# Other durations in the model by which a hybrid decoder layer's instructions are put in order

## The chip, the core and the metric

The kernel runs on one core of one Trainium2 chip. Its time is device microseconds (us) of that core, from the first instruction to the last, for one launch that computes the whole step. A core has the engines PE (TensorE, matmuls and transposes; its weight loads are listed apart as PEld), DVE (VectorE), ACT (ScalarE), POOL (GpSimd) and SP (SyncE, which here issues nearly all DMA transfers). Each engine works through its own list of instructions strictly in the order in which the program holds them, and waits at an instruction until the semaphores it names have been raised by the others.

## What is computed

One layer of a hybrid decoder, for a prompt of 512 tokens with 16 learned meta tokens ahead of it, and for 8 sequences that decode one token each (536 tokens in all, width 1024):

```
h  = RMSNorm(x)
x += W_o( sig(gate_a) * W_a(GatedDeltaNet(h)) + sig(gate_b) * W_b(GLA(h)) )
x += W_down( gelu(causal_dwconv3(RMSNorm(x) W_up)) * (RMSNorm(x) W_gate) )
y  = RMSNorm(x)
```

`h @ w_in` is a product with 7192 output columns that gives queries, keys, values and gates of both mixers. The delta mixer (4 heads of 128) works in chunks:

```
M = where(strict, (k*beta) k^T * decay, 0);  T = inverse(I + M)       # triangular solve
u = T (v*beta);  w = T (k*beta*exp(G));  v_new = u - w S
o = (q*exp(G)) S + (q k^T * decay) v_new;  S = S*exp(gl) + (k*exp(gl-G))^T v_new
```

The GLA mixer (4 heads, 128x256 state) does the same without the inverse but with a decay per key column. The ConvFFN has 2816 hidden columns. The decode samples take one recurrent step on the states given. Everything is float32; new states and convolution rows are returned too.

## The kernel before

**Big products.** Each is cut into jobs of 128 output columns. A job loads its weights by DMA into a tile `wr` (128x8x128, three buffers), splits each half of it into a rounded part `wh` (cast, ACT) and the rest `wl` (subtraction, DVE; four buffers each), and adds up `hTh*wh + hTl*wh + hTh*wl` in a PSUM tile `g`. These are matmuls of 128x128 weights on 260 to 268 columns; a job with 1024 rows of weights is 48 of them. When it is complete, its result is evacuated, for the columns of `w_in` by ACT or DVE into `zt` and from there to DRAM (`z_d`). The jobs' `g` tiles share few buffers, so a later job can begin only when an earlier one's tile has been evacuated. The second half of the program is the ConvFFN, which is hardly anything but such jobs.

**Small work.** The mixers' chunk work is cut into many small matmuls (16, 32, 64 or 128 rows or columns) into PSUM tiles `s`, with transposes (`tr`, by a matmul with the identity). They are threaded into the stream of the jobs. The inverse is done in two stages. For all 16 diagonal blocks of 32x32 at once DVE solves row by row: 31 pairs of `tensor_tensor`, a product `tmpb<-Ab,Xb` and a sum `Xb<-Xb,tmpb`, each on the result of the one before. The blocks come to it by DMA through DRAM (`nb_d`, `Ab`), and its results go back by DMA through DRAM: four `xb_d<-Xb` and then four `NT<-xb_d`. From there PE combines blocks of 32 to 64 (`s<-NT 32x32`, `s<-Uu,Pm`) and of 64 to 128 (`s<-NT 64x64`, `s<-Uu,Pg`), with copies by ACT (`Pm`, `Pg`, `Uu`) and transposes by DVE (`Uu<-NT`) between the steps; then the chunks follow one after another.

**What sets the order.** Nothing is issued while the body runs. Each operation is recorded by `Plan.add` with its engine, a modelled cost, a latency `lat` (0.17 unless given) and a priority (a due time by a simple clock of `Driver`). `Plan.emit`, called twice (once for the mixers, once for the FFN), then plays the whole program through in time: it takes the engine that is free first, and among its operations whose inputs are there (`need`) the one of the highest priority; it models the SP queue, the ACT tables, PE's two clocks, the rotation of buffers, and a charge where PE goes from full-size to small operations (0.09) or back (0.3). The order of start times found is the order in which each engine's instructions stand in the program. So a modelled duration changes nothing that is computed; it can only move an instruction ahead of or behind others. `need` is set in two places, at L183 (inputs that an earlier `emit` already placed) and at L265 (all others): the time at which the input's operation is modelled to be finished, `lat` included, and without `lat` if both are on PE.

**Where the modelled costs are.** `mm` (L414) and `tr` (L425) give PE's. All operations of the other engines get theirs in `Engine` (L360).

Of the kernel before, what the change touches and what calls it, by code (L numbers as in the profile page):

```python
# [16 lines left out]
P = 128  # L17
# [58 lines left out]

class Op:
    __slots__ = ("eng", "cost", "lat", "fn", "pri", "func", "need", "deps", "users", "tiles", "finish", "left", "duty", "small", "lock", "hold")


def boxes(ap):
# [36 lines left out]
class Plan:  # L118
# [50 lines left out]
    def emit(self):  # L169
# [4 lines left out]
        for op in ops:  # L174
            op.left = 0
            if op.eng in ("sync", "gpsimd"):
                op.need = op.pri[0] - 100.0
            for d in op.deps:
                if d.finish is None:
                    op.left += 1  # L180
                    d.users.append(op)
                else:
                    op.need = max(op.need, d.finish - (d.lat if d.eng == op.eng == "PE" else 0.0))  # L183

        def offer(op):
            for n in op.tiles:
                if n not in alloc:
                    waiting[self.tag[n]].setdefault(n, []).append(op)
                    return
                op.need = max(op.need, alloc[n])  # L190
            cand.setdefault(op.eng, []).append(op)

        def grant(tag):
            while self.next[tag] < len(self.order[tag]) and self.slots[tag]:
                n = self.order[tag][self.next[tag]]
                self.slots[tag].sort()
                alloc[n] = self.slots[tag].pop(0)
                self.next[tag] += 1
                for op in waiting[tag].pop(n, []):
                    offer(op)  # L200
# [7 lines left out]
        while len(done) < len(ops):  # L208
            best = None
            for e, l in cand.items():  # L210
                if l:
                    t = max(self.free.get(e, 0.0), min(o.need for o in l))
                    if best is None or t < best[0]:
                        best = (t, e)
            if best is None:
                raise RuntimeError("no instruction can go on")
            t, e = best
            able = [o for o in cand[e] if o.need <= t + 0.01]
            if e == "PE" and self.idle > 0.3:
                able = [o for o in able if o.duty > 0.9 * o.cost] or able  # L220
            op = min(able, key=lambda o: o.pri)
            if e == "PE" and op.small != self.small:

                same = [o for o in able if o.small == self.small and (self.small or t < op.need + op.hold)]
                op = min(same, key=lambda o: o.pri) if same else op
            if e in WAITERS:
                soon = [o for o in cand[e] if o.pri[0] < op.pri[0] - 2.0 and o.need < t + WF * op.cost]
                if soon:
                    op = min(soon, key=lambda o: o.need)
                    t = max(t, op.need)  # L230
            cand[e].remove(op)
            cost = op.cost
            if e == "sync":
                t = max([t, self.hw] + self.queue[-8:-7])
                self.hw = t + 0.475
                self.bw = max(self.hw + 0.65, self.bw) + cost
                op.finish = self.bw + 0.9
                self.queue.append(op.finish)
                self.free[e] = max(t + 0.06, self.hw - 0.3)
            else:  # L240
                if op.func and not (self.set and op.func in self.set):
                    s = [x for x in ACT_SETS if op.func in x]
                    if s:
                        cost += 1.28
                        self.set = s[0]
                if e == "PE":
                    while t >= self.tick + 3.413:
                        self.warm, self.cols, self.tick = self.cols >= 1.275, 0.0, self.tick + 3.413
                    self.cols += op.duty
                    self.idle = max(self.idle + 0.5 * (t + cost - self.free.get(e, 0.0)) - op.duty, -0.3)  # L250
                    if self.small != op.small:
                        cost += TO_PARTS if op.small else TO_WHOLE
                    self.small = op.small
                    if not self.warm:
                        cost += op.duty
                if op.lock:

                    t = max(t, self.port[e == "vector"])
                    self.port[e != "vector"] = t + cost
                self.free[e] = t + cost  # L260
                op.finish = t + cost + op.lat
            done.append((t, len(done), op))
            for u in op.users:
                u.left -= 1
                u.need = max(u.need, op.finish - (op.lat if op.eng == u.eng == "PE" else 0.0))  # L265
                if u.left == 0:
                    offer(u)
            for n in op.tiles:
                live[n] -= 1
                if live[n] == 0:  # L270
                    tag = self.tag[n]
                    if n not in self.held:
                        self.slots[tag].append(op.finish)
                        grant(tag)
# [119 lines left out]
def body(ctx, tc, I, O):  # L394
    nc = tc.nc
    drv = Driver()
# [17 lines left out]
    def mm(out, lhsT, rhs, start=True, stop=True):  # L414
        n, m = rhs.shape[-1], lhsT.shape[-1]
        k = lhsT.shape[0]
        small = rhs.dtype != F32R and (m <= 64 or k <= 64)
        if rhs.dtype == F32R:
            cost = max(n / 2400 + .0117, .112 * m / P, .025)
        else:  # L420
            cost = n / 2400 + .005 if m <= 32 or k <= 32 else .058 if m <= 64 and n <= 64 else max(n / 600 + .005, .222 * m / P)
        duty = (n / 2400 if rhs.dtype == F32R else n / 2400 + .007 if m <= 32 else n / 600) * k / P
        drv.matmul(cost, out, [lhsT, rhs], lambda: nc.tensor.matmul(out=out, lhsT=lhsT, rhs=rhs, start=start, stop=stop), duty, small)  # L423

    def tr(out, in_):  # L425
        k = in_.shape[0]
        drv.matmul(max(.03, .110 * k / P), out, [in_], lambda: nc.tensor.transpose(out, in_, ident[:k, :k]), 2 * k / 2400 * k / P, k <= 64)  # L427

    def S_(name="s"):
        p, n = ps_pool[-1]  # L430
# [116 lines left out]
    def run(jobs, W):  # L547
        while jobs:
# [11 lines left out]
            for bs in ((0,), (1,)) if len(group) > 1 else (range(group[0].nb),):  # L560
                for j, ps in zip(group, acc):
                    n, K = 0, sum(k for _, k in j.srcs)
                    cols = halves(j.c0, j.n) if j.halves else spans(j.c0, j.n) if j.nb > 1 else [(0, j.n)]

                    pv = ps.rearrange("p a b -> p (a b)")[:, 512 - cols[0][1]:][:, :j.n] if j.nb > 1 else ps[:, 0, :j.n]
                    for i, (s, kk) in enumerate(j.srcs):
                        if (j, i) not in ws:
                            ws[j, i] = W.next()
                        for k in range(kk):
                            hi, lo = ws[j, i][k // 4]  # L570
                            ah, al = j.acts(n + k)
                            drv.poll(drv.earliest(hi, lo, ah, al, *([ps] if n + k == 0 else [])))
                            for p, (w, a) in enumerate(((hi, ah), (hi, al), (lo, ah))):
                                for b in bs:
                                    mm(pv[:j.M, cols[b][0]:cols[b][1]], w[:, k % 4, :j.M], a[:, j.c0 + cols[b][0]:j.c0 + cols[b][1]],
                                       start=n + k == 0 and p == 0, stop=n + k == K - 1 and p == 2)
                        n += kk
                    if bs[-1] == j.nb - 1:
                        with ahead(EV):
                            j.evac(pv[:j.M])  # L580
                        drv.poll()
# [4 lines left out]
    ident = cst[:, C_ID:C_ID + P]  # L586
# [76 lines left out]
    def warm_up():  # L663

        ps = S_("warm")
        for _ in range(28):
            mm(ps[:, :P], scm[:, :P], scm[:, :P])

    def turn_weights():
        ps = S_()  # L670
        tr(ps[:, :8], nmr)
        dve.tensor_copy(nrm_mix, ps[:, :8])
# [55 lines left out]
    def small_operands():  # L728
# [21 lines left out]
        for m in range(12):  # L750
            tr(ps[:, m * 28:(m + 1) * 28], csr[:28, m * P:(m + 1) * P])
# [1074 lines left out]
```

## Time and profile before

| | |
|---|---|
| time, median of 3 runs | 986.65 us (986.44 to 990.56) |
| the profiled execution | 986.13 us, its span 984.4 us |
| granted TensorE clock, mean over the span | 0.995 of full speed |
| PE busy | 968.4 us |
| DVE / ACT / POOL busy | 606.6 / 463.3 / 185.3 us |
| DMA | 135.48 MB, 138 GB/s over the span |

Matmuls are pipelined, so a row of the timeline shows a start and the time until the end of the last of its matmuls, which reaches past the start of the next row. What a matmul takes of PE's time is the distance from start to start. In brackets stands the time in which the engine did nothing ahead of the instruction, and what ended it. Of float32 matmuls with small tiles the trace holds two records for one instruction.

### The profile page before, as it was taken

What the parts mean: (1) busy time and instruction counts of PE and PEld (TensorE: products, weight loads), DVE (VectorE), ACT (ScalarE), POOL (GpSimd) and SP (SyncE); (2) the same over time, 40 slices, a digit from 0 to 9 for tenths busy, and PEclk for the clock granted to TensorE, in tenths of its full rate; (3) what the DMA queues carried; (4) which work ended last, traced back from release to release, by engine and by line L of the source; (5) the groups of instructions that cost most, each with busy time, mean ns of one, the idle gap of its engine ahead of it and who ended that gap; (6) DMA issues with size and microseconds to landing.
All of it is one profiled execution on the core that took longest, in us unless ns stands there. A gap on an engine that the chain in (4) does not pass through costs nothing.

```text
span 984.4 us, 21968 instructions
## 1 busy us (share of the span) xinstructions
PE 968.4 (98%) x9022; PEld 950.4 (97%) x9022; DVE 606.6 (62%) x1197; ACT 463.3 (47%) x905; POOL 185.3 (19%) x278
## 2 busy tenths in 40 slices
PE   9999999999999999999999999999999999999996
PEld 8999999998999999999999999999999999999996
DVE  4879867883457867324754447777776766433254
ACT  6566654745446455244643337344443433232343
POOL 4100116101222244012211122111122111000000
PEclk9999999999999999999999999999999999999998
DMA  7643322445123232656655536477655554433354
GB/s 235 184 116 88 87 66 65 133 130 142 34 77 87 79 90 83 188 161 204 204 174 150 162 110 182 139 237 213 199 157 156 166 152 126 126 118 93 111 143 140
DMA packets 208681, 135.48 MB, mean 138 GB/s; under 512 B 14353, under 2 KB 196392, under 8 KB 208308
## 3 DMA queue, kind: packets, MB, share of 16 engines
q1 hardware_dynamic: 208580, 134.07, 46.9%
q8 instruction: 71, 1.16, 0.5%
q14 instruction: 30, 0.25, 0.1%
HBM read 112.26 MB, written 21.98 MB: 136 GB/s over the span
## 4 chain that ended last, share of the span: by engine, by line
PE 81%; DMA 1%; issue 0%; DVE 0%; ACT 0%; SPq 0%; POOLq 0%; POOL 0%; ACTq 0%
PE g L423 71%; PE s L423 8%; PE s L427 1%; DMA xb_d<-Xb 0%; DMA NT<-xb_d 0%; PE on L423 0%; ACT zt L389 0%; PE pk L423 0%; SPq L389 0%; PE pq L423 0%; POOLq L1822 0%; ACT gat L389 0%; DVE wy L389 0%; DVE ga L389 0%; POOL rfb L389 0%
## 5 line engine op out<-in xcount | busy, mean ns | idle before, releaser
L389 ACT CAST wh<-wr 128x512 fp32r<-128x512 f32 (+1 forms) x300 | 183.1, 612 | 312.3 <-PE g L423 297.4
L389 DVE TENSOR_TENSOR wl<-wr,wh 128x512 fp32r<-128x512 f32 (+1 forms) x296 | 203.6, 698 | 177.1 <-ACT wh L389 175.4
L423 PE MATMUL g<-hTh,wh 128*128 128x268 f32 (+3 forms) x768 | 160.8, 288 | 1.0 <-ACT zt L389 1.0
L423 PE MATMUL g<-hTl,wh 128*128 128x268 f32 (+3 forms) x768 | 161.7, 288 | 0.0
L423 PE MATMUL g<-hTh,wl 128*128 128x268 f32 (+3 forms) x768 | 160.9, 288 | 0.0
L423 PE MATMUL g<-h2l,wh 128*128 128x260 f32 x704 | 142.8, 284 | 0.0
L423 PE MATMUL g<-h2h,wh 128*128 128x260 f32 x704 | 142.0, 282 | 0.0
L423 PE MATMUL g<-h2h,wl 128*128 128x260 f32 x704 | 142.0, 283 | 0.0
L423 PEld LDWEIGHTS g<-hTh,wh 128*128 128x128 f32 x768 | 120.0, 189 | 3.6 <-issue 1.9
L423 PEld LDWEIGHTS g<-hTl,wh 128*128 128x128 f32 x768 | 120.9, 189 | 1.7 <-issue 1.2
L423 PEld LDWEIGHTS g<-hTh,wl 128*128 128x128 f32 x768 | 119.8, 189 | 1.5 <-issue 1.2
L423 PEld LDWEIGHTS g<-h2h,wl 128*128 128x128 f32 x704 | 109.3, 189 | 0.1
L423 PEld LDWEIGHTS g<-h2h,wh 128*128 128x128 f32 x704 | 108.6, 189 | 0.1
L423 PEld LDWEIGHTS g<-h2l,wh 128*128 128x128 f32 x704 | 108.6, 189 | 0.0
L423 PE MATMUL g<-actl,wh 128*128 128x260 f32 (+2 forms) x352 | 79.3, 284 | 0.0
L423 PE MATMUL g<-acth,wh 128*128 128x260 f32 (+2 forms) x352 | 78.2, 283 | 0.0
L423 PE MATMUL g<-acth,wl 128*128 128x260 f32 (+2 forms) x352 | 77.9, 282 | 0.0
L423 PEld LDWEIGHTS g<-actl,wh 128*128 128x128 f32 x352 | 57.7, 188 | 0.1
L423 PEld LDWEIGHTS g<-acth,wl 128*128 128x128 f32 x352 | 57.3, 188 | 0.0
L423 PEld LDWEIGHTS g<-acth,wh 128*128 128x128 f32 x352 | 57.2, 188 | 0.0
L389 ACT ACT_TABLE_LOAD x34 | 43.6, 1283 | 7.4 <-DVE na L389 3.4
L389 POOL TENSOR_TENSOR E<-kb,E 128x256 f32<-128x256 f32 (+1 forms) x32 | 25.5, 807 | 56.5 <-DVE E L389 31.9
(362 smaller groups left out, 1675.5 us busy)
## 6 DMA issues: line engine op xcount, KB each, us to landing
wr<-in_w_in SPq DMA_DIRECT2D x56, 512.0 KB
wr<-in_w_ffn_in SPq DMA_DIRECT2D x44, 512.0 KB
wr<-in_w_ffn_out SPq DMA_DIRECT2D x20, 512.0 KB
z_d<-zt SPq DMA_DIRECT2D x28, 261.0 KB
Sg<-in_state_gla SPq DMA_DIRECT2D x8, 512.0 KB
wr<-in_w_b_out SPq DMA_DIRECT2D x8, 512.0 KB
wr<-in_w_o SPq DMA_DIRECT2D x8, 512.0 KB
So<-in_state_gla SPq DMA_DIRECT2D x8, 512.0 KB
```

Source lines behind the costliest of these rows:

```text
L389: self.drv.issue(self.key, cost, out, ins, 2.2 if self.key == "sync" else 0.17, lambda: f(*args, **kw), func, lock)
L423: drv.matmul(cost, out, [lhsT, rhs], lambda: nc.tensor.matmul(out=out, lhsT=lhsT, rhs=rhs, start=start, stop=stop), duty, small)
L427: drv.matmul(max(.03, .110 * k / P), out, [in_], lambda: nc.tensor.transpose(out, in_, ident[:k, :k]), 2 * k / 2400 * k / P, k <= 64)
```

## The change

A function `Op.saved` says by how much earlier than others a user on the same engine sees a result. On PE this is `lat`, as before. On DVE, ACT and POOL it is `lat` less 0.03, where nothing was taken off before; for users on another engine, and for SP, nothing, as before. It stands in both places at which `need` is set. The cost of float32 matmuls on PE is changed for operands of 64 or fewer rows or columns: with 32 or fewer contraction rows (`k`) and more than 32 output rows (`m`) the cheap formula no longer holds, and a 64x64 product is set to 0.12 instead of 0.058. A transpose costs at least 0.05 instead of 0.03.

```diff
+    def saved(self, user):
+
+        return 0.0 if user.eng != self.eng or self.eng == "sync" else self.lat - (0.0 if self.eng == "PE" else 0.03)
...
-                    op.need = max(op.need, d.finish - (d.lat if d.eng == op.eng == "PE" else 0.0))
+                    op.need = max(op.need, d.finish - d.saved(op))
...
-                u.need = max(u.need, op.finish - (op.lat if op.eng == u.eng == "PE" else 0.0))
+                u.need = max(u.need, op.finish - op.saved(u))
...
-            cost = n / 2400 + .005 if m <= 32 or k <= 32 else .058 if m <= 64 and n <= 64 else max(n / 600 + .005, .222 * m / P)
+            cost = n / 2400 + .005 if m <= 32 else .12 if m <= 64 and n <= 64 else max(n / 600 + .005, .222 * m / P if k > 32 else 0.0)
...
-        drv.matmul(max(.03, .110 * k / P), out, [in_], lambda: nc.tensor.transpose(out, in_, ident[:k, :k]), 2 * k / 2400 * k / P, k <= 64)
+        drv.matmul(max(.05, .110 * k / P), out, [in_], lambda: nc.tensor.transpose(out, in_, ident[:k, :k]), 2 * k / 2400 * k / P, k <= 64)
```

The instructions themselves stay the same, but for two more loads of an ACT table (36 instead of 34). Their order changes on every engine. On PE it changes in the mixers' part; from the last jobs of that part on, which is from about 487 us of the span before, the order on PE is the same row for row. Lines below L80 stand 4 further down in the changed kernel (L389, L423, L427 become L393, L427, L431).

SP, at the end of the diagonal blocks' solve. `xb0` to `xb3` carry the solve's results to DRAM, `NT` brings them back, `z7` and `z8` are the results of the jobs with tiles `g_547` and `g_554`, `wr` the weights of later jobs, `er_d` a row of the decode samples. Before:

```order
L389 DMA z7_d_78<-zt_553 128x522
L389 DMA wr_555<-in_w_in 128x8x128
L389 DMA z8_d_79<-zt_562 128x522
L389 DMA xb0_d_125<-Xb_410 16x1024
L389 DMA xb1_d_126<-Xb_410 16x1024
L389 DMA xb2_d_127<-Xb_410 16x1024
L389 DMA xb3_d_128<-Xb_410 16x1024
L389 DMA wr_564<-in_w_in 128x8x128
L389 DMA NT_405<-xb0_d_125 32x16x32
```

And now:

```order
L393 DMA wr_555<-in_w_in 128x8x128
L393 DMA xb0_d_125<-Xb_410 16x1024
L393 DMA xb1_d_126<-Xb_410 16x1024
L393 DMA xb2_d_127<-Xb_410 16x1024
L393 DMA z7_d_78<-zt_553 128x522
L393 DMA xb3_d_128<-Xb_410 16x1024
L393 DMA wr_564<-in_w_in 128x8x128
L393 DMA NT_405<-xb0_d_125 32x16x32
L393 DMA NT_405<-xb1_d_126 32x16x32
L393 DMA NT_405<-xb2_d_127 32x16x32
L393 DMA er_d_107<-err_546 32x128
L393 DMA NT_405<-xb3_d_128 32x16x32
```

The four `xb` stood behind `z8`; now three of them stand ahead of `z7` and the fourth behind it, and `z8` (not shown) comes after the last `NT`.

PE, where one job of `w_in` ends while the next ones run (`g_554`, `g_563` and `g_575` are three jobs that follow each other). Before:

```order
L423 MATMUL g_554<-hTh_68,wl_552 128x262
L423 MATMUL g_554<-hTh_68,wl_552 128x260
L423 MATMUL g_575<-hTh_68,wh_565 128x262
L423 MATMUL g_575<-hTh_68,wh_565 128x260
L423 MATMUL g_575<-hTl_69,wh_565 128x262
L423 MATMUL g_575<-hTl_69,wh_565 128x260
L423 MATMUL g_563<-hTh_68,wl_557 128x262
L423 MATMUL g_563<-hTh_68,wl_557 128x260
```

And now:

```order
L427 MATMUL g_554<-hTh_68,wl_552 128x262
L427 MATMUL g_554<-hTh_68,wl_552 128x260
L427 MATMUL g_563<-hTh_68,wh_556 128x262
L427 MATMUL g_563<-hTh_68,wh_556 128x260
L427 MATMUL g_563<-hTl_69,wh_556 128x262
L427 MATMUL g_563<-hTl_69,wh_556 128x260
```

Before, `g_563` had been begun within `g_554`, so that at the end of `g_554` the job after next was begun; now the jobs run one after another. The same is moved in the jobs of the mixers' output products, where `ohb` is the operand of the second mixer: its job was interleaved with the one before it and now runs alone.

PE, at the second stage of the inverse (`NT`, `Uu`, `Pg`: its 64x64 blocks; `meta,Um__174`: the meta tokens' part). Before, with `s<-NT 64x64` standing 27 matmuls further up:

```order
L423 MATMUL g<-hTh,wh 128x262
L423 MATMUL g<-hTh,wh 128x260
L423 MATMUL g<-hTl,wh 128x262
L423 MATMUL s<-Uu,Pg 64x64 x16
L423 MATMUL s<-meta,Um__174 16x128 x4
L423 MATMUL g<-hTl,wh 128x260
```

And now:

```order
L427 MATMUL g<-hTl,wh 128x262
L427 MATMUL g<-hTl,wh 128x260
L427 MATMUL g<-hTh,wl 128x262
L427 MATMUL s<-NT 64x64 x16
L427 MATMUL s<-Uu,Pg 64x64 x16
L427 MATMUL s<-meta,Um__174 16x128 x4
L427 MATMUL g<-hTh,wl 128x260
```

Three blocks that were apart now form one.

## Rows read from the trace of the kernel before

**Rows 1.** The page: busy time of each engine, and the last chain by engine.

```profile
PE 968.4 (98%) x9022; PEld 950.4 (97%) x9022; DVE 606.6 (62%) x1197; ACT 463.3 (47%) x905; POOL 185.3 (19%) x278
...
PE 81%; DMA 1%; issue 0%; DVE 0%; ACT 0%; SPq 0%; POOLq 0%; POOL 0%; ACTq 0%
```

**Rows 2.** Busy time by windows of 25 us: window, its length, then each engine.

```profile
core 0: us, PE busy (x) PEld busy (x) DVE busy (x) ACT busy (x) POOL busy (x), PEclk, DMA share, GB/s
...
475.00:500.00 25.00, 24.21 (x200) 24.00 (x199) 16.33 (x26) 13.82 (x24) 8.20 (x6) 1.00 0.63 192
...
700.00:725.00 25.00, 25.00 (x210) 25.00 (x209) 19.92 (x36) 9.35 (x19) 4.98 (x10) 1.00 0.57 169
```

**Rows 3.** Timeline of PE: start, duration, instruction, count, idle before and releaser.

```profile
163.69 0.49 PE L423 MATMUL pk<-kT 128*128 128x128 f32 x2 [0.36 <-DVE NT L389]
...
216.92 0.51 PE L423 MATMUL g<-hTh,wh 128*128 128x262 f32 x2 [0.27 <-ACT zt L389]
...
223.72 0.51 PE L423 MATMUL g<-hTh,wh 128*128 128x262 f32 x2 [0.74 <-ACT zt L389]
...
231.16 0.24 PE L423 MATMUL s<-NT 32*32 32x32 f32 x2 [0.28 <-DMA NT<-xb_d]
231.92 0.66 PE L423 MATMUL s<-NT 32*32 32x32 f32 x30 [0.52 <-DMA NT<-xb_d]
...
317.07 0.36 PE L423 MATMUL s<-nst,sel 128*128 128x260 f32 x1 [0.39 <-DVE atd L389]
...
394.68 0.35 PE L423 MATMUL s<-qb,kb 128*32 128x32 f32 x18 [1.00 <-issue]
...
485.02 0.50 PE L423 MATMUL g<-ohb,wh 128*128 128x260 f32 x2 [0.79 <-DVE ga L389]
```

**Rows 4.** Timeline of PE, one small matmul between full ones.

```profile
234.35 0.41 PE L423 MATMUL g<-hTh,wl 128*128 128x262 f32 x2
234.60 0.40 PE L423 MATMUL g<-hTh,wh 128*128 128x262 f32 x2
234.93 0.24 PE L423 MATMUL s<-Uu,Pm 32*32 32x32 f32 x2
235.10 0.51 PE L423 MATMUL g<-hTl,wh 128*128 128x262 f32 x2
235.44 0.41 PE L423 MATMUL g<-hTh,wl 128*128 128x262 f32 x2
```

**Rows 5.** Timeline of DVE: the solve's first two steps and its last.

```profile
178.14 0.19 DVE L389 TENSOR_TENSOR tmpb<-Ab,Xb 68x31 f32<-68x31 f32 x1 [1.36 <-DMA Ab<-nb_d]
178.36 0.21 DVE L389 TENSOR_TENSOR Xb<-Xb,tmpb 68x31 f32<-68x31 f32 x1
...
217.50 0.19 DVE L389 TENSOR_TENSOR Xb<-Xb,tmpb 68x31 f32<-68x31 f32 x1
```

**Rows 6.** Chain that ended last, 170 to 240 us: start, duration, piece.

```profile
223.06 0.61 ACT zt L389
223.69 0.32 SPq L389
...
224.10 3.56 DMA xb_d<-Xb
...
228.66 3.21 DMA NT<-xb_d
```

**Rows 7.** PE and its granted clock, by windows around the one fall.

```profile
250.00:253.70 3.70, 3.70 (x63) 1.00 0.02 4
253.70:257.10 3.40, 3.40 (x17) 0.50 0.41 106
```

**Rows 8.** Timeline of PE: the blocks of the inverse's second stage.

```profile
239.27 2.08 PE L423 MATMUL s<-NT 64*64 64x64 f32 x32
...
244.73 2.07 PE L423 MATMUL s<-Uu,Pg 64*64 64x64 f32 x32
246.74 1.04 PE L423 MATMUL s<-meta,Um__174 16*16 16x128 f32 x8
```

## The prediction

> **What bounds the kernel now.** I read the page's busy times and its last chain first: PE is busy for 968.4 of 984.4 us, DVE for 62%, ACT for 47%, and the chain that ended last is PE's by 81% [rows 1]. So the time is what PE needs for its list plus its gaps, and a reordering can only win where PE waits or where its order costs time of its own. The table of windows then says where that is: in a window of the ConvFFN PE is busy for all of 25.00 us with 210 records, while the window at the end of the mixers' part has 24.21 [rows 2]. PE's order is the same in both kernels from 487 us on, so I take the second half as fixed and look at the first alone. There the timeline of PE names the waits [rows 3]; the eight listed are all those after 40 us that are more than a pipeline's ripple, and they come to 0.36 + 0.27 + 0.74 + 0.28 + 0.52 + 0.39 + 1.00 + 0.79 = 4.35 us. Last I read the solve on DVE [rows 5] and the chain that follows it [rows 6], since the change speaks of DVE's results, and the granted clock, which fell once to 0.50, the lower of its two levels (1.2 of 2.4 GHz), for 3.40 us [rows 7] and so cost about 1.7 us.
>
> **The change, part by part.** *Own results after 0.03.* The solve shows the true distance on DVE: the first step lasts 0.19 us from 178.14, and the next one, which reads it, starts at 178.36, 0.03 later [rows 5]. The old model put 0.17 there, so over the 62 steps it had the solve end 62 x 0.14 = 8.7 us later than its durations allow. The planner therefore put what follows, the reads of the solve's results, further down than needed. Nothing gets faster on DVE by this; what moves is where the reads stand on PE and SP. On ACT and POOL I have no row for the same thing; between nothing and the old 0.17 for an operation, both engines lie far from full [rows 1], so I cost their reordering at nothing, with DVE's and ACT's idle time as its cover. The two table loads more on ACT go with that: ACT has over half of the span free, and only a `zt` or `wh` that comes late on the path would show them.
>
> *Waits of PE for a job's buffer.* At 216.92 and 223.72 PE waits for ACT to evacuate the job that has just ended, since the next job had already been begun within it and it is the one after that which needs the buffer: 0.27 and 0.74 us [rows 3]. In the new order the jobs run one after another, and a job takes the buffer of the one before the last, which has had a whole job of 48 matmuls at 0.12 us, 5.8 us, to be evacuated in; the evacuation lasts 0.61 [rows 6]. At 485.02 the same happens with DVE's `ga`, 0.79 us, and there too the interleaving is gone. I take all three as removed: -1.80. Next in line there are the `wl` halves of the jobs that follow, on an engine that is free for over a third of the span [rows 1].
>
> *Waits for the solve's way back.* PE waits 0.28 and 0.52 us for `NT` [rows 3]. The solve ended at 217.50 + 0.19 = 217.69 [rows 5], yet the first `xb_d` was issued only at 224.10, because `z_d` stood ahead of it and waited for the evacuation begun at 223.06 [rows 6]. In the new order three `xb_d` stand ahead of `z7` and the last behind it. On PE the first `s<-NT` stands behind 1457 matmuls of jobs instead of 1500 (counted in the two orders), 43 x 0.12 = 5.2 us earlier, near 226.8. Does the data make it? `z7` belongs to `g_547`, which ends 48 + 17 matmuls, 65 x 0.12 = 7.8 us, before `s<-NT`. From there: evacuation 0.61, issue 0.32, the last `xb_d` 3.56, an issue of 0.32, `NT` 3.21: 8.0 us [rows 6]. That is a wait of 0.2; I take 0.3 instead of 0.80: -0.50. The bounds are -0.8 (none) and, if it lands as late as now, +5.2, which is a rival below.
>
> Here the Trainium skill differs from the rows. Its page "DMA: Bandwidth & Descriptors", under "Anatomy of one DMA", gives a transfer a fixed cost of about 2.0 us, fitted there to transfers that GpSimd issues, while these are issued by SP; by that the two transfers would take 4 us and the wait would be gone, -0.8 in place of -0.50. The rows have 3.56 and 3.21 for these two, and the measurement decides.
>
> *Other waits.* 163.69 and 317.07 (0.36 and 0.39) are small matmuls that stand too close behind a DVE result, and 394.68 (1.00) is a wait that the trace puts down to nothing in particular [rows 3]. In the new order other instructions stand around all three, but nothing shows that they are far enough off. Between none and all of 1.75 I take half: -0.9. On the other side, the reads of the inverse, of the GLA tiles and of the samples' states now stand 4 to 16 us earlier by the count of matmuls ahead of them, so some will meet a result that is not quite there. The nearest rows are waits of this very kind, 0.28 and 0.39; I take two: +0.7, with 0 and the 5.2 above as bounds.
>
> *Fewer visits to small tiles.* One small matmul alone between full ones costs this: from 234.60 to 235.44 are 0.84 us, in which four full matmuls lie; a pair takes 0.25 (234.35 to 234.60), so 0.84 - 0.50 = 0.34 are left for one 32x32 matmul [rows 4]. I put the visit itself at 0.3. In the new order separate runs of fp32 matmuls on part of the array fall from 34 to 30 (`s<-Uu,Pg` behind `s<-NT 64x64` is one of those joined): 4 x 0.3 = -1.2. Runs of short transposes go from 38 to 39; they need no term, since runs of full size cost no visit. Bounds 0 and -1.6.
>
> The Trainium skill says in "TensorEngine Tiling (Array Packing)", under Key Properties, that a change of the tiling mode, not only of the tile, drains TensorE. The visit above agrees. But the rule also speaks against part of the gain: where a run of 64x64 is joined to one of another tile size, a drain stays between them. If that holds for two of the four, half of their 0.3 each comes back, and the term is -0.9.
>
> *The clock.* It fell after a run of 16-row matmuls; that run stands together in the new order as well, so I keep one fall, term 0. It could be none (-1.7) or more: the joined block of the second stage is now 2.08 + 2.07 + 1.04, about 5 us in one piece, where pieces of 2.1 and 3.1 us stood [rows 8] and no fall followed them.
>
> **Sum.** -1.80 - 0.50 - 0.9 + 0.7 - 1.2 = -3.7, against the profiled execution's 986.13 (a span of 984.4 and 1.7 around it): 982.4. The median shown, 986.65, lies 0.52 above that execution, so the forecast for a median is 982.9.
>
> **Rivals.**
>
> All of it goes. No new wait, all 4.35 us of waits removed, the visits' 1.2, and no fall of the clock: -7.3, so 979.4. For it: the orders are wider exactly where waits stood. Against it: half of the removed waits are argued from places, not from durations.
>
> The waits change place. The planner now packs by new numbers, and what it gains at old places it loses at new ones: only -1.2 is left, 985.4. That the change does nothing on the path at all (986.6) lies next to it. For it: each wait in the list is under 1.1 us, and the model is no finer than that; against it: the three buffer waits are removed by construction.
>
> The inverse comes late, the one that ends slower. It hangs on one place, the fourth `xb_d` behind `z7` on SP. If the evacuation or the transfers take so long that `NT` lands when it does now, about 231.9, PE, which stands there 5.2 us earlier, waits for all of that: 982.9 + 5.2 = 988.1. It decides once the landing slips by more than 3.7 us beyond the sum above. For it: a transfer of 3.56 us is slow already and the first half is the one with heavy weight traffic. Against it: evacuation and reads are both tied to PE's own progress, and 8.0 us stands against 7.8.
>
> More falls of the clock. Two more, at 1.7 each, behind the joined small blocks: 986.3. For it: the fall seen came behind small matmuls. Against it: 3.1 us of them in one piece passed without one [rows 8].
>
> **How the numbers follow.** The forecast's own case (981 to 985) gets 0.45, all goes 0.22, the waits change place 0.17, the inverse late 0.09, more falls 0.07. A measurement of this kernel tells about 0.5% from no change, 4.9 us, so faster is below 981.7 and slower above 991.6. Faster: 0.22 and a third of the forecast's case, 0.37. Slower needs the late inverse and something beside it, such as a fall of the clock in PE's wait: 0.05. The rest, 0.58, is the same. The range reaches from below "all goes" to just over the late inverse, 978.0 to 988.5, which leaves some 0.08 below and 0.08 above.
>
> **What would show it.** In the new profile: PE's waits for `zt` near 217 and 224 and for `ga` near 485 absent (if they stand at other jobs, the waits have changed place); `xb_d` issued close behind the solve's last step and PE's first `s<-NT` near 226 with under 1 us of wait (over 3 us: the late inverse); the FFN windows at 25.00 us with 210 records; one window at 0.50. PE's busy time should fall by 1 to 2 us through the visits, and the rest of the gain should be idle time. I am wrong if PE's idle time before 487 us is not smaller than now, or if the second half differs by more than half a us, since I hold that part to be fixed.

## The result and the profile after

The changed kernel takes 981.92 us (median of 5 runs, 980.47 to 982.68) where the kernel before takes 986.65 (5 runs, 984.61 to 990.56). The ratio is 0.9941, 95% interval 0.9924 to 0.9958: faster by 0.6%, clear of no change. Whether it is more than the 0.5% that the prediction asks of "faster" is not settled: the interval lies on both sides of it, and 981.92 just above the 981.7 named there. In a later comparison with other runs of the kernel before the ratio was 0.9932 (0.9915 to 0.9950). The forecast was 982.9, a gain of 3.7 us. By the medians the gain is 4.7, by the two ratios 5.8 (4.1 to 7.5) and 6.7 (4.9 to 8.4), so the forecast was too small. The profiled execution took 982.36 us, 3.77 less than the profiled one of before, where the sum of the prediction had 3.7; that these two agree so closely is partly luck, as shown below.

The page after, in the parts of [rows 1]:

```profile
PE 966.8 (99%) x9022; PEld 949.8 (97%) x9022; DVE 606.3 (62%) x1197; ACT 466.8 (48%) x907; POOL 184.2 (19%) x278
...
PE 92%; DVE 2%; DMA 2%; SPq 1%; issue 1%; ACT 1%; POOL 0%; POOLq 0%; ACTq 0%
```

PE's busy time fell by 1.6 us (968.4 to 966.8). The span fell by 3.9 (984.4 to 980.5), so the other 2.3 us are idle time. The windows, as in [rows 2] and [rows 7]; the first is the stretch in which the clock was low after the change:

```profile
core 0: us, PE busy (x) PEld busy (x) DVE busy (x) ACT busy (x) POOL busy (x), PEclk, DMA share, GB/s
244.30:247.70 3.40, 3.40 (x18) 3.40 (x17) 2.55 (x9) 0.00 (x0) 0.00 (x0) 0.51 0.02 5
475.00:500.00 25.00, 25.00 (x209) 25.00 (x209) 10.68 (x17) 10.71 (x18) 4.86 (x3) 1.00 0.48 144
600.00:625.00 25.00, 24.61 (x204) 24.40 (x204) 22.88 (x39) 12.70 (x25) 6.49 (x12) 1.00 0.41 115
700.00:725.00 25.00, 25.00 (x211) 25.00 (x210) 16.68 (x30) 9.68 (x19) 5.98 (x9) 1.00 0.54 161
```

The window that had 24.21 of 25.00 us busy is full now. A new hole stands at the beginning of the ConvFFN, 600 to 625. The clock fell once, for the same 3.4 us. PE's waits, as in [rows 3]:

```profile
21.42 0.33 PE L431 MATMUL s<-cst,xu 128*128 128x128 f32 x1 [0.98 <-DVE xr L393]
...
169.49 0.36 PE L427 MATMUL s<-lrR,gkR 80*128 80x268 f32 x1 [0.17 <-DVE NT L393]
...
225.18 0.31 PE L427 MATMUL s<-NT 32*32 32x32 f32 x7 [0.31 <-DMA NT<-xb_d]
...
349.85 0.35 PE L427 MATMUL s<-eD,Sg 128*128 128x128 f32 x1 [0.34 <-POOL kp L393]
...
409.56 0.42 PE L427 MATMUL s<-Sg,zw 128*32 128x256 f32 x4 [0.63 <-DMA Sg<-in_state_gla]
...
609.51 0.39 PE L427 MATMUL g<-h2h,wh 128*128 128x260 f32 x1 [0.39 <-DVE gl L393]
```

The three waits for a job's buffer (`zt` at 217 and 224, `ga` at 485) are gone, as are those at 317 and 395. Three of the rows are new: 0.34 for POOL's `kp`, 0.63 for the samples' states `Sg`, 0.39 for `gl`. The end of the solve on DVE and what SP does behind it, as in [rows 5] and [rows 6]:

```profile
216.05 0.19 DVE L393 TENSOR_TENSOR Xb<-Xb,tmpb 68x31 f32<-68x31 f32 x1
```

```profile
216.27 1.25 SPq L393 DMA_DIRECT2D xb_d<-Xb  x3
217.61 0.37 SPq L393 DMA_DIRECT2D z_d<-zt  x1
218.02 0.44 SPq L393 DMA_DIRECT2D xb_d<-Xb  x1
...
222.54 0.42 SPq L393 DMA_DIRECT2D NT<-xb_d  x1
```

The first `xb_d` is issued 0.03 us after the solve's last step. Before, it was issued 6.4 us after it (217.69 to 224.10), behind `z_d`.

### The profile page after: what moved, and what is told of

Same layout as the page of the kernel before. It is cut to its first block, busy times and chain, and to the rows that moved or that the text cites. A ratio compares the mean times of both kernels' runs of the same rounds, so it can differ in the third digit from the quotient of the medians.

```text
span 980.5 us, 21967 instructions
## 1 busy us (share of the span) xinstructions
PE 966.8 (99%) x9022; PEld 949.8 (97%) x9022; DVE 606.3 (62%) x1197; ACT 466.8 (48%) x907; POOL 184.2 (19%) x278
## 4 chain that ended last, share of the span: by engine, by line
PE 92%; DVE 2%; DMA 2%; SPq 1%; issue 1%; ACT 1%; POOL 0%; POOLq 0%; ACTq 0%
PE g L427 81%; PE s L427 8%; PE s L431 2%; SPq L393 1%; DMA xu<-in_x_prompt 1%; DMA Sg<-in_state_gla 1%; DMA NT<-xb_d 0%; PE pk L427 0%; PE pq L427 0%; DVE fy L393 0%; DVE wl L393 0%; ACT L393 0%; DVE gkR L393 0%; ACT wh L393 0%; PE pd L431 0%
## 5 line engine op out<-in xcount | busy, mean ns | idle before, releaser
L393 ACT CAST wh<-wr 128x512 fp32r<-128x512 f32 (+1 forms) x300 | 183.2, 612 | 312.0 <-PE g L427 301.7
L393 DVE TENSOR_TENSOR wl<-wr,wh 128x512 fp32r<-128x512 f32 (+1 forms) x296 | 202.9, 694 | 176.1 <-ACT wh L393 165.0
L427 PE MATMUL g<-hTh,wh 128*128 128x268 f32 (+3 forms) x768 | 163.5, 290 | 0.0
L427 PE MATMUL g<-hTl,wh 128*128 128x268 f32 (+3 forms) x768 | 160.4, 287 | 0.0
L427 PE MATMUL g<-hTh,wl 128*128 128x268 f32 (+3 forms) x768 | 159.5, 287 | 0.0
L427 PE MATMUL g<-h2l,wh 128*128 128x260 f32 x704 | 142.8, 284 | 0.0
L427 PE MATMUL g<-h2h,wh 128*128 128x260 f32 x704 | 142.1, 283 | 0.4 <-DVE gl L393 0.4
L427 PE MATMUL g<-h2h,wl 128*128 128x260 f32 x704 | 141.9, 283 | 0.0
L427 PEld LDWEIGHTS g<-hTh,wh 128*128 128x128 f32 x768 | 120.7, 189 | 1.4 <-issue 1.0
L427 PEld LDWEIGHTS g<-hTh,wl 128*128 128x128 f32 x768 | 119.6, 188 | 2.0 <-issue 1.9
L427 PEld LDWEIGHTS g<-hTl,wh 128*128 128x128 f32 x768 | 120.2, 189 | 1.4 <-issue 1.0
L427 PEld LDWEIGHTS g<-h2h,wl 128*128 128x128 f32 x704 | 109.3, 189 | 0.0
L427 PEld LDWEIGHTS g<-h2h,wh 128*128 128x128 f32 x704 | 108.6, 189 | 0.6 <-DVE gl L393 0.6
L427 PEld LDWEIGHTS g<-h2l,wh 128*128 128x128 f32 x704 | 108.6, 189 | 0.0
L427 PE MATMUL g<-actl,wh 128*128 128x260 f32 (+2 forms) x352 | 79.3, 284 | 0.0
L427 PE MATMUL g<-acth,wh 128*128 128x260 f32 (+2 forms) x352 | 78.2, 283 | 0.0
L427 PE MATMUL g<-acth,wl 128*128 128x260 f32 (+2 forms) x352 | 77.9, 282 | 0.0
L427 PEld LDWEIGHTS g<-actl,wh 128*128 128x128 f32 x352 | 57.7, 188 | 0.1
L427 PEld LDWEIGHTS g<-acth,wl 128*128 128x128 f32 x352 | 57.3, 188 | 0.0
L427 PEld LDWEIGHTS g<-acth,wh 128*128 128x128 f32 x352 | 57.2, 188 | 0.0
L393 DVE SCALAR_TENSOR_TENSOR fy<-up,fT,fy 128x536 f32<-128x536 f32 x44 | 35.1, 798 | 1.6
```

What stands on the lines that cost most here:

```text
L393: self.drv.issue(self.key, cost, out, ins, 2.2 if self.key == "sync" else 0.17, lambda: f(*args, **kw), func, lock)
```

## The experiments

All ratios are against runs of the kernel before on the same chip. A profile shows one execution of a kernel; the times of executions differ more than some of the effects below.

**The parts of the change, one at a time.** The changed kernel with PE's old costs, so that only the rule on own results is left:

```diff
-            cost = n / 2400 + .005 if m <= 32 else .12 if m <= 64 and n <= 64 else max(...)
+            cost = n / 2400 + .005 if m <= 32 or k <= 32 else .058 if m <= 64 and n <= 64 else max(...)
-        drv.matmul(max(.05, .110 * k / P), ...)
+        drv.matmul(max(.03, .110 * k / P), ...)
```

> The rule on own results alone, with PE's costs as before. Theory (waits go by the rule on own results, visits to small tiles by PE's costs): the order has the jobs g_554, g_563, g_575 in a row and the xb transfers ahead of z8, as in the changed kernel, but 33 runs of small tiles instead of 34. So PE's idle time falls by some 2 us from the 6.2 us of before, its busy time by less than 0.5: 984.2, ratio 0.9975. Rival 1 (all comes from PE's costs): 986.6 with the waits at 217, 224 and 231 still there. Rival 2 (all comes from the rule on own results): 982, ratio 0.995.

The kernel before with PE's new cost of small matmuls alone:

```diff
-            cost = n / 2400 + .005 if m <= 32 or k <= 32 else .058 if m <= 64 and n <= 64 else max(...)
+            cost = n / 2400 + .005 if m <= 32 else .12 if m <= 64 and n <= 64 else max(...)
```

> The cost of small fp32 matmuls alone; own results and transposes as before. Theory: SP's order around the solve and the begun-early jobs stay as before, so the waits at 217, 224, 231 and 232 stay (1.8 us); 29 runs of small tiles instead of 34 take 5 x 0.3 = 1.5 us off PE's busy time: 985.1, ratio 0.9985. Rival 1 (all comes from PE's costs): 982, ratio 0.995. Rival 2 (all from own results): 986.6.

Measured: own results alone 0.9955 (0.9938 to 0.9971), small matmuls alone 0.9971 (0.9952 to 0.9989). Both rivals fall: each part does something by itself. Own results did more than I expected (0.9975); the 0.9985 expected of the small matmuls lies within their interval. The new rule alone leaves one of the three waits for a job's buffer (PE of that kernel):

```profile
480.17 0.39 PE L427 MATMUL g<-ohb,wh 128*128 128x260 f32 x1 [0.80 <-DVE ga L393]
```

In the profile of the small matmuls alone no wait for `ga` is left, although the two output products are still interleaved there in part. So this wait goes with PE's new cost. The waits at 317 and 395 of [rows 3] are absent there too, 2.18 us with `ga`'s; a wait of 0.84 for `Sg` and one of 0.34 for `gl` are new. With five visits less (1.5) that makes 2.5 us, an estimate from two executions, for a measured 2.9 (1.1 to 4.7). The waits for `zt` and `NT` stand where they stood, but those for `NT` are far longer than in [rows 3]:

```profile
232.10 0.24 PE L423 MATMUL s<-NT 32*32 32x32 f32 x2 [1.96 <-DMA NT<-xb_d]
232.93 0.34 PE L423 MATMUL s<-NT 32*32 32x32 f32 x10 [0.58 <-DMA NT<-xb_d]
```

and behind them the granted clock falls (windows of the same kernel: PE's busy time, then its clock):

```profile
230.00:235.00 5.00, 2.46 (x67) 0.82 1.06 208
235.00:240.00 5.00, 5.00 (x111) 0.50 0.49 124
240.00:245.00 5.00, 5.00 (x42) 0.66 0.01 3
245.00:250.00 5.00, 5.00 (x63) 1.00 0.01 2
```

This execution took 989.70 us, the slowest of that kernel's twelve. That is about 10 us at the low clock, some 5 us lost, behind 2.5 us of waiting. The kernel before varies in the same way: in its 29 executions beside this run the mean clock lies between 0.992 and 0.998; the seven at 0.992 took 990.4 to 992.1 us, the five at 0.998 took 985.0 to 986.2. The execution that I had read took 986.13 us, and only six of the 29 took less. The mean clock also counts time that costs nothing: in each profile here the clock falls to 0.50 behind PE's last matmul, 4 to 7 us before the span ends (at 977.3 of 984.4 us in the kernel before). So the profile at 0.995 has only one fall within PE's work.

**The solve alone.** In the kernel before, only the 62 operations of the diagonal solve get the short latency:

```diff
+            drv.own = 0.03
             tt(tv, bcl(Av[:, j, j + 1:], w), bch(Xv[:, j, :w], n), MUL)
             tt(Xv[:, j + 1:, :w], Xv[:, j + 1:, :w], tv, SUB)
+            drv.own = 0.17
...
-        self.plan.add(key, cost, fn, out, ins, self.t - self.lead, func, lock=lock)
+        self.plan.add(key, cost, fn, out, ins, self.t - self.lead, func, lock=lock, lat=self.own)
```

> The shorter latency for the 62 operations of the diagonal solve alone, all else as before. Theory (the solve is what the rule on own results is about): PE's first s<-NT stands behind 1462 matmuls of jobs instead of 1500, z8 is no longer ahead of the xb transfers, and the 0.8 us of waits for NT shrink to about 0.3; of the waits for zt at least one is left, since three jobs are still begun within another: 985.4, ratio 0.999. Rival (the other own results on DVE, ACT and POOL matter as much): the same 985.4 here, but the run with the whole rule is over 1 us better than this one.

Measured 0.9958 (0.9941 to 0.9975), by the ratio as much as the whole rule, and more than the 0.999 expected. Its profile differs from the expectation in two places: both waits for `zt` are gone, where I had left at least one, and the wait for `NT` has not shrunk but is 0.80 us in one piece:

```profile
224.81 1.19 PE L424 MATMUL s<-NT 32*32 32x32 f32 x62 [0.80 <-DMA NT<-xb_d]
```

The rival, that the other own results matter as much, stays open: by the medians (984.95 and 982.82 us) the whole rule is 2.1 us better, by the ratios (0.9958 and 0.9955) next to nothing.

**The solve's way back, with nothing else moved.** After planning, `z8` is put behind the four `xb_d` on SP; every other engine's order is that of before:

```diff
-        for t, _, op in sorted(done, key=lambda x: x[:2]):
-            op.fn()
+        row = [op for t, _, op in sorted(done, key=lambda x: x[:2])]
+        xb = [i for i, op in enumerate(row) if op.eng == "sync" and op.to.startswith("xb")]
+        if xb:
+            z = max(i for i in range(xb[0]) if row[i].eng == "sync")
+            row.insert(xb[-1], row.pop(z))
+        for op in row:
+            op.fn()
```

> The kernel before with one DMA moved: z8 stands behind the four xb transfers on SP instead of ahead of them; every other engine's order is as before. Theory (PE's wait for the solve's way back costs its 0.8 us of idle time, and in some executions, where it is longer, the granted clock falls behind it and PE pays for 3 to 10 us at half speed): the waits at 231 and 232 are gone, no low clock begins between 231 and 245, the runs' mean clock no longer goes down to 0.992, and the median is 1 to 3 us below the kernel before: ratio 0.998. Rival (the clock falls for the small matmuls' sake, whatever PE waited): only the 0.8 us, ratio 0.9992, with clocks as before.

Measured 0.9968 (0.9957 to 0.9980): one DMA, put behind four others, is 3.2 us (2.0 to 4.2). SP, and the windows of PE:

```profile
217.10 2.11 SPq L395 DMA_DIRECT2D xb_d<-Xb  x4
223.03 0.34 SPq L395 DMA_DIRECT2D z_d<-zt  x1
...
223.96 3.95 SPq L395 DMA_DIRECT2D NT<-xb_d  x4
```

```profile
230.00:235.00 5.00, 5.00 (x127) 1.00 0.88 238
235.00:240.00 5.00, 5.00 (x123) 1.00 0.13 37
240.00:245.00 5.00, 5.00 (x58) 1.00 0.56 158
```

PE reaches `s<-NT` at 230.14 without a wait, and the clock stays up through the blocks that follow, the same matmuls in the same order as in the kernel before.

How much of the 3.2 us is the wait, and how much the clock? Six profiles have this order on PE with `z8` ahead of the `xb_d`: that of the kernel before, that of the transposes alone and the four with extra matmuls (both below). Their two waits for `NT` add up to 0.80, 1.78, 1.60, 1.95, 1.81 and 2.14 us, 1.7 in the mean. The one that I had read is the smallest by half. So the wait alone accounts for some 1.7 of the 3.2 us, by estimate.

The clock does not follow the wait strictly. In the five of these with 1.60 us or more it fell within 2 us behind the wait in three, each time for 3.4 us, and not in the other two. With one 32x32 matmul added in the ConvFFN (PE's first wait for `NT`, then its windows):

```profile
231.39 0.24 PE L429 MATMUL s<-NT 32*32 32x32 f32 x2 [1.09 <-DMA NT<-xb_d]
230.00:235.00 5.00, 3.40 (x75) 3.04 (x74) 3.50 (x5) 1.70 (x4) 0.52 (x1) 0.82 1.04 206
235.00:240.00 5.00, 5.00 (x119) 4.54 (x119) 2.58 (x12) 2.65 (x6) 0.69 (x3) 0.84 0.41 107
```

With two of them, behind a longer wait:

```profile
232.22 0.24 PE L429 MATMUL s<-NT 32*32 32x32 f32 x2 [1.55 <-DMA NT<-xb_d]
230.00:235.00 5.00, 3.05 (x78) 2.69 (x77) 2.71 (x4) 1.80 (x4) 0.52 (x1) 1.00 1.08 216
235.00:240.00 5.00, 5.00 (x125) 4.64 (x124) 3.76 (x17) 3.67 (x8) 0.69 (x3) 1.00 0.59 128
```

In the eight profiles with 0.80 us of wait or none, this one among them, no fall came within 10 us; six of them have one later, so a fall does not need this wait either. The eleven executions have a mean clock of 0.9964 (0.995 to 0.998), the 22 of the kernel before beside them 0.9956 (0.992 to 0.998). Over 985 us that is about 0.7 us. So most of the gain is the wait, and the clock has the smaller part. The rival as I wrote it, with 0.8 us, is excluded; with 1.7 us for the wait it would be at 0.9983, only just outside the interval, so the clock's part is likely rather than shown.

**Transposes alone.** The kernel before with this one cost:

```diff
-        drv.matmul(max(.03, .110 * k / P), ...)
+        drv.matmul(max(.05, .110 * k / P), ...)
```

> The longer cost of short transposes alone. Theory (it wins nothing on PE, and at the start of the program, where xu and xr are turned, it spreads the transposes so that one waits for DVE's xr): PE's time up to 42 us is 1 to 2 us longer than in the runs with the old cost, with a wait of about 1.0 for xr near 21; the rest as before: 1.001. Rival (the late start in the two profiles of the changed cost came from that execution's transfers): start as in the others, no difference, 1.000.

Measured 1.0020 (1.0005 to 1.0035): alone, this part makes the kernel slower, by little. PE of that kernel:

```profile
20.80 0.33 PE L427 MATMUL s<-cst,xu 128*128 128x128 f32 x1 [0.98 <-DVE xr L389]
```

The wait for `xr`, 0.97 or 0.98 us, stands in all four profiles of kernels with the new cost (two of the changed kernel, this one, and the next), and of the profiles with the old cost only the first of before has one there (0.78 at 20.27). PE comes to its first matmul of `hTh` at 73.5 to 74.6 us in these four and at 72.2 to 73.3 in the other ten, so the start is later, as expected. That this is what the 0.2% (2.0 us) consists of is not shown: the mean clock of these executions is 0.9947 against 0.9956, about 0.9 us by itself, and this profile has the long waits for `NT`, as before.

**The ConvFFN planned by the old rule.** The changed kernel, in which the rule on own results ends where the ConvFFN begins:

```diff
+OLD = []
-        return 0.0 if user.eng != self.eng or self.eng == "sync" else self.lat - (...)
+        return 0.0 if user.eng != self.eng or self.eng == "sync" or OLD and self.eng != "PE" else self.lat - (...)
...
     pb.close()
+    OLD.append(1)
```

> The changed kernel, with own results reckoned as before in the second plan, the ConvFFN's. PE's order is that of the changed kernel throughout; on DVE the gl product stands ahead of the wl subtraction again at the beginning of the ConvFFN. Theory (the new wait of 0.39 us for gl near 609 comes from that exchange): the wait is gone, FFN time as before the change, 0.45 us less than the changed kernel: 981.5, ratio 0.9945. Rival (the wait comes from the earlier start of the ConvFFN, with other transfers in flight): it stays, 981.9.

Measured 0.9927 (0.9905 to 0.9949), 980.26 us. DVE of the changed kernel and then of this one, at the beginning of the ConvFFN:

```profile
605.72 2.52 DVE L393 SCALAR_TENSOR_TENSOR fy<-up,fT,fy 128x536 f32<-128x536 f32 x2
608.16 0.68 DVE L393 TENSOR_TENSOR wl<-wr,wh 128x512 fp32r<-128x512 f32 x1
608.76 0.69 DVE L393 TENSOR_TENSOR gl<-g,gl 128x520 f32<-128x520 f32 x1
```

```profile
604.66 2.52 DVE L396 SCALAR_TENSOR_TENSOR fy<-up,fT,fy 128x536 f32<-128x536 f32 x2
607.10 0.69 DVE L396 TENSOR_TENSOR gl<-g,gl 128x520 f32<-128x520 f32 x1
607.71 0.68 DVE L396 TENSOR_TENSOR wl<-wr,wh 128x512 fp32r<-128x512 f32 x1
```

The subtraction of 0.6 us ahead of `gl` is gone, and with it PE's wait: the step at this matmul, against the kernel before, is 0.25 us instead of 0.55. But the ConvFFN did not get faster. From the first `g<-h2h` to PE's end it takes 387.52 us here, and 387.48 and 387.52 in two profiles of the changed kernel; before, it was 386.99. The 0.45 us expected are not there. Nor does the wait need the exchange: the profile of the small matmuls alone has `gl` ahead of `wl` and a wait all the same (DVE, then PE):

```profile
616.01 0.68 DVE L389 TENSOR_TENSOR gl<-g,gl 128x520 f32<-128x520 f32 x1
616.62 0.67 DVE L389 TENSOR_TENSOR wl<-wr,wh 128x512 fp32r<-128x512 f32 x1
616.75 0.51 PE L423 MATMUL g<-h2h,wh 128*128 128x260 f32 x2 [0.34 <-DVE gl L389]
```

There the ConvFFN takes 387.70 us, with the old rule. Kernels with the old order on DVE thus span 386.99 to 387.70, so the 0.5 us that the second half of the changed kernel seems to lose is no more than executions differ by.

**Both at once, and the changed kernel again beside it.** The changed kernel without the new cost of transposes and with the old rule in the ConvFFN (the two edits above):

> The changed kernel without the new cost of transposes, and with own results as before in the second plan. If the start is lost by the transposes' cost (1.0 to 1.5 us) and the ConvFFN's wait by the second plan (0.3): 980.3 - 1.3 = 979.0 where the changed kernel has 981.9, ratio to the changed kernel 0.997. If the rival holds for the start: as the run with the second plan alone, 980.3.

> The changed kernel again, on the chip and against the same runs as the other three: 981 to 982.5, ratio 0.994, mean clock 0.995 to 0.997 in every run (no execution at 0.992, as the kernel before has them).

Measured 0.9926 (0.9908 to 0.9943), 980.66 us, and for the changed kernel 0.9932 (0.9915 to 0.9950), 980.82. The wait for `xr` is gone from the profile as expected and its span is 979.0 against 981.2. The medians do not show it: 980.66 is near the 980.3 that I had named for the rival, not 979.0. Neither this version nor the one before it is shown to beat the changed kernel, whose mean clocks are 0.995 to 0.997, as expected.

**What a visit to a small tile costs.** 88 extra matmuls in the ConvFFN's first product, in the 12th and 36th place of each of its 44 jobs, in the kernel before:

```diff
+            nc.tensor.matmul(out=out, lhsT=lhsT, rhs=rhs, start=start, stop=stop)
+            if ps is not None:
+                nc.tensor.matmul(out=ps[:32, 0, 0:32], lhsT=cst[:32, :32], rhs=cst[:32, :32], start=False, stop=False)
```

> The kernel before, with 88 extra 32x32 fp32 matmuls, each alone between two full-size ones of the ConvFFN's first product (two in each of its 44 jobs); their results lie in unused columns and are never read. Theory (a visit to a small tile costs about 0.3 us beside the matmul's own 0.04): 88 x 0.34 = +30 us. Rival (a visit costs only its own issue, 0.1 us or less, and the 0.34 of the trace was a wait): under +9 us.

> As v1, with two 32x32 matmuls next to each other in each of the 88 places. Theory (the visit is what costs): 88 x 0.38 = +33 us, only 3 more than v1. Rival (each small matmul costs the same wherever it stands): twice the extra time of v1.

> As v1, with a 64x64 matmul and behind it a 32x32 one in each of the 88 places. Theory (a change between two small tile sizes costs little; the visit costs 0.3, the 64x64 matmul 0.12, the other 0.04): 88 x 0.46 = +40 us. Rival (each change of the tiling drains the engine alike): 0.15 more each, 88 x 0.61 = +54 us.

> As v1, but the extra matmul is full-size: 128x128 fp32 weights on 32 columns, so no other tile. Theory: no visit, only the matmul's own time, between 0.06 (its columns) and 0.22 (its weights): 88 x 0.14 = +12 us, well under v1 although it does 16 times the work. Rival (any extra fp32 matmul among rounded ones costs the switch): as v1, +30 us.

I take the time from the first `g<-h2h` to the first `g<-act` matmul of each profile, which holds all 88 places and no low clock. It is 254.97 us before (up to 255.67 in other profiles without extra matmuls, 0.008 us per place), and with the extra matmuls:

| extra in each place | time | more, per place |
|---|---|---|
| one 32x32 | 287.46 | 0.369 |
| two 32x32 | 292.43 | 0.426 |
| 64x64, then 32x32 | 308.56 | 0.609 |
| one 128x128 on 32 columns | 274.39 | 0.221 |

The first and the third, in PE's timeline:

```profile
701.67 0.41 PE L429 MATMUL g<-h2h,wl 128*128 128x260 f32 x2
702.01 0.24 PE L431 MATMUL g<-cst 32*32 32x32 f32 x2
702.18 0.51 PE L429 MATMUL g<-h2h,wh 128*128 128x260 f32 x2
```

```profile
702.51 0.33 PE L431 MATMUL g<-cst 64*64 64x64 f32 x2
702.76 0.24 PE L432 MATMUL g<-cst 32*32 32x32 f32 x2
702.94 0.39 PE L429 MATMUL g<-h2h,wh 128*128 128x260 f32 x1
```

A second small matmul adds 0.057 us, so the visit itself is 0.31 by difference. Going on from 64x64 to 32x32 adds 0.24 to a visit, of which the 64x64 matmul itself takes 0.13 by the blocks of [rows 8] (2.08 us for 16 of them): some 0.11 are left for the change between two small tiles. That is an estimate: no run has the 64x64 matmul alone, so a dearer way in or out of 64x64 tiles is not excluded. The expectation without such a drain (0.46) is off, the rival's 0.61 is met. A full-size fp32 matmul on the same 32 columns costs less than a 32x32 one, but with 0.221 more than the 0.14 that I expected; it lies between that and the rival's 0.34.

## Why the prediction was right, and where not

*Own results.* Right: nothing on DVE got faster (606.6 and 606.3 us busy), and reads and transfers moved. PE's idle time before 487 us fell from 7.1 to 4.4 us. The solve alone gave as much as the whole rule by the ratios; whether the other results add to it is open.

*Waits for a job's buffer, -1.80.* Right in size and place: all three are absent in both profiles of the changed kernel. The third is not own results' doing: it stands with that rule alone (0.80) and is absent with the small matmuls' cost alone.

*The solve's way back, -0.50.* This is the term that was mis-sized. The working itself held: PE came to `s<-NT` at 224.6, the last of the transfers made it wait for 0.31 (0.80 in the second profile), where I had 0.3. But I priced what it replaces by one execution with 0.8 us, the smallest of six; the others have 1.6 to 2.1. Moving that one DMA is worth 3.2 us (2.0 to 4.2), by estimate some 1.7 for the wait and 0.7 for the granted clock. The rival in which the inverse comes late fell: the transfers landed as worked out.

*Other waits, -0.9, and new ones, +0.7.* 0.36, 0.39 and 1.00 became one of 0.17, so -1.58, and the new ones are 0.34 + 0.63 + 0.39 = 1.36. Both terms were half of what came, and the two errors cancel (-0.22 for -0.2), which is luck. It is also one execution: the wait for `Sg` is 0.63, 0.43 and nothing in three profiles with this order on PE. The waits for `Sg` and for `kp`, a tile of the GLA mixer, are of the kinds I had named; `gl` is not.

*Visits, -1.2.* PE's busy time fell by 1.6, and a visit measured by itself costs 0.31 where I had 0.3. The rule on tiling changes that I took from the Trainium skill's "TensorEngine Tiling (Array Packing)", Key Properties, agrees with the runs: a change between two small tile sizes seems to cost, though with 0.11 less than half a visit. The small matmuls alone gave 2.9 us (1.1 to 4.7) where five visits less make 1.5; the waits that go and come in their profile make up another 1.0.

*The clock, 0.* In the two profiles that I compare it fell once in each, so the term is right there. Over executions it is not: 0.992 to 0.998 before, 0.995 to 0.997 after. In the later comparison the means are 0.9956 and 0.9963, about 0.7 us. So the clock gives part of the gain beyond 3.7 us; another part is the solve's way back, mis-sized as above. Whether the two make up all of it is not shown.

*Transposes, no term.* Wrong: alone they cost 0.2%, and the start is later with them, which I had left out by looking at the waits after 40 us only. The reason that I gave for no term, that such runs are full-size, does not fit the trace either: the short transposes of the kernel before hold weights on 8 to 36 of 128 rows. That the start is the whole cost is not shown, and taking them out of the changed kernel showed no gain.

*The second half fixed.* Right as far as can be told: the changed kernel is 4.35 us ahead of the profile of before when the ConvFFN begins, and 3.87 when it ends, just under the half us that I had set as a bound. PE's order was the same, but DVE's was not. The wait for `gl` goes with that, yet without it the ConvFFN took as long.

## What to carry to other kernels

Do not price a wait for a transfer by one execution: the same wait was 0.8 us in the profile that I had read and 1.6 to 2.1 in five others. A wait of PE can cost more than its idle time, since the clock may fall behind it, but it need not: compare the mean clocks of many executions, and find in a profile which falls lie within PE's work. A wait that is gone from a profile is not yet time won; read the time of the whole stage beside it, as with `gl` here. When the constants of a planner are brought to measured values, try each by itself: here two of three helped, and the third, alone, cost a little.

## What the runs showed of the hardware

In the run with the small matmuls' cost alone PE waited 1.96 and 0.58 us, and the granted clock fell to 0.50 within the next microsecond and stayed there for some 10 us, through a stretch of small and full-size matmuls in which PE was busy all the time. In the order of the kernel before it fell for 3.4 us within 2 us behind waits of 1.60, 1.78 and 2.14 us, and did not fall behind 1.81 and 1.95. A 32x32 fp32 matmul alone among full-size ones cost 0.37 us, a 128x128 one on as many columns 0.22, and a change between 64x64 and 32x32 about 0.11, by estimate.
